# Order of the last group's down products, pinned operand splits and earlier loads in an encoder layer's MLP

## The chip, the cores and the metric

The kernel runs on one core of a Trainium2 chip. The metric is the device time of one execution in microseconds. TensorE (PE in the profile) multiplies matrices, VectorE (DVE), ScalarE (ACT) and GpSimd (POOL) work on elements, and SyncE (SP) issues most transfers (DMAs); GpSimd issues those transfers that add into their destination.

## The reference

One layer of an encoder on 1024 tokens of 1024 channels, in fp32, and what matters here is its gated MLP (D_FF = 2816):

```python
hn = rmsnorm(h, norm_ffn_g[i])
up = hn @ w_up[i]
gt, val = up[..., :D_FF], up[..., D_FF:]
gt = causal_dwconv(gt, conv_w[i], conv_b[i])
h = h + (jax.nn.gelu(gt, approximate=False) * val) @ w_down[i]
...
gate = jax.nn.sigmoid(hn @ w_ple_gate[i] + b_ple_gate[i])
h = h + gate * (p[i] @ w_ple[i])
```

Before it stand a pooling mixer, a chunked attention and the output projection.

## The kernel before, in words

Every fp32 product is made of three matmuls of fp32r halves (`mm3`, L128 to L130: high by high, high by low, low by high). An operand is first *split*: ScalarE copies it to its high half (L133), VectorE subtracts that for the low half (L134). The order of TensorE's instructions is the program's; on the other engines a scheduler orders them, by the data they wait for and by a priority (`tc.high_priority` puts an instruction ahead). SP and GpSimd work their queues of transfers strictly in the resulting order.

The MLP works in 22 tiles `fi` of 128 of D_FF's channels. Both of its products are made by a seven-product scheme for two by two blocks (Strassen's, in a form that needs few sums), so that seven block products stand for eight; they are numbered 1 to 7.

*Up products.* For a tile, step `n` is product `n` of the block scheme, 12 matmuls of 128x512. `order` lists all steps: four are done ahead, those of tile 0 follow in the order 6 3 7 4, of tile 1 in 5 6 2 7 3 4, of the others in 1 5 6 2 7 3 4. `prepare` makes the operand of a step up to four steps ahead: `fetch` loads the blocks of w_up into six buffers `rawu` (L695), as many steps ahead as its argument says and as far as buffers are free; `summed` adds blocks on VectorE (L699), then the operand is split. `step` runs the twelve matmuls into a bank of PSUM and then what follows: `keep` (L784) copies a bank to SBUF, `seed` (L788) copies a bank to another as the start of its sum, `gate` makes the convolution on ScalarE and VectorE (L833 to L835) and the Gelu (L836), `values_in` multiplies gate and value (L841, L843). Tiles in `halved` do the gate in two halves of 512 tokens, the others in one of 1024. The first Gelu needs another table of ScalarE's functions, loaded just before it.

*Down products.* The finished rows of tiles 0 to 19 are stored in DRAM (`Yd`), and w_down's product over them is made in five groups `g` of four tiles. Product `(g, n)` has 24 matmuls. Its operands are sums of quarters of w_down and `Yd`, made by the transfers: `ask` loads the first part plainly from SP and adds the others by accumulating DMAs of GpSimd (both recorded at L942 or L940), into the buffers RW. Products 5, 6 and 3 have buffers of their own in which the sum *grows*: product 6 adds to what product 5 had, and product 3 to that of 6 on the side of w_down. The others share one set. A buffer is asked anew when its last product has been split, and a row of `Yd` only when its tile is stored (`stored`). `split_next` splits the operands of the next product (L133 and L134, and L972 and L973 where the sign is turned), into the tiles BQ and four pieces of R; `down_next` runs the product, adds the four results to the residual (L990), and calls `split_next` for the one after. The hooks of `up` place one or more down products between the steps of a tile (`downs`). Products of a group go in the order 1 2 5 4 6 7 3.

*The end of the MLP.* Tiles 20 and 21 need no DRAM; their w_down rows, and the operands of the product of p and w_ple, are late pieces, loaded and split through the `rawu` buffers by `late_pair` (L1041), in hooks of tile 21 and after it. The last group's seven products lie in tiles 19 (three of them), 20 and 21.

Of the kernel before, what the change touches and what calls it, by code (L numbers as in the profile page):

```python
# [59 lines left out]
DOWN_ORDER = (1, 2, 5, 4, 6, 7, 3)  # L60
# [33 lines left out]
def trunk(tc, xT, pT, vecs, w_qk0, w_in, w_v, bias, counts, pool_w, w_out, w_up, w_down,  # L94
# [4 lines left out]
    with tc.tile_pool(name="sb", bufs=1) as sb, \  # L99
# [32 lines left out]
        def split(src, hi, lo):  # L132
            act.activation(hi, src, AF.Copy)  # L133
            dve.tensor_tensor(lo, src, rv(hi), ALU.subtract)  # L134
# [506 lines left out]
        out_weights(0, pooled)  # L641
        norm_a = Norm(HS[0], tmp[0], tmp[2:3], 6, 6)
# [28 lines left out]
        steps = {0: (6, 3, 7, 4), 1: (5, 6, 2, 7, 3, 4)}  # L671
# [29 lines left out]
        def prepare(upto):  # L701
            while prepared[0] < min(upto, len(order)):
                fi, n = order[prepared[0]]
                w_ = wu[prepared[0] % 3]
                prepared[0] += 1
                fetch(prepared[0] + 3)
                assert fetched[0] == len(loads) or loads[fetched[0]][0] >= prepared[0]
                if (fi, n) in alone:
                    t, = done_with = [held[(fi, n), q] for q in FORMS[n]]
                else:  # L710
                    a11, a12, a21, a22 = [held.get((fi, q)) for q in ((0, 0), (0, 1), (1, 0), (1, 1))]
                    if n == 5:
                        summed(a21, a21, a22)
                    elif n == 6:
                        summed(a21, a21, a11)
                    elif n == 3 and not fi:
                        summed(a11, a21, a12)
                    elif n == 7:
                        if fi:
# [3 lines left out]
                    done_with = {3: [a11, a12], 7: [a21], 4: [a22]}.get(n, []) if fi == 0 else {  # L723
                        3: [a11], 7: [a12, a21], 4: [a22]}.get(n, [])
# [55 lines left out]
        halved = (1, NF - 1)  # L780
# [9 lines left out]
        def step(fi, n):  # L790

            x, y, z, w = firsts.get(fi, (0, 1, 2, 3))
            product({1: x, 2: x, 5: z, 3: z, 6: y, 7: y, 4: w}[n], n in (1, 5) or (fi, n) == (0, 4))
# [16 lines left out]
            elif n == 7:  # L810
                if fi:
                    seed(w, y)
                else:
                    keep(V[:, HS[0]], y)
                dve.tensor_tensor(V[:, HS[1]], PS[:, y], p5, ALU.subtract)
            elif n == 4:
                if fi:
# [20 lines left out]
        def values_in(ts, negative=None):  # L838
# [6 lines left out]
            for h in range(2):  # L845
                y = Yb[:, HS[h]]
# [30 lines left out]
        def up(fi, dst, hooks=None):  # L877
# [30 lines left out]

        def sources(side, g, n):

            for j in range(2):
                if side == "w":
                    yield j, [w_down[group_of(g)[2 * k + j], :, i * 512:(i + 1) * 512] for i, k in DOWN_W[n]]
                else:
                    yield j, [Yd[group_of(g)[2 * k + j]][:, HS[t]] for k, t in DOWN_A[n]]
# [4 lines left out]
        def ask():  # L920
# [3 lines left out]
            for side in "wa":  # L924
                for kind in ("one", "grow"):
                    queue = todo_of[side, kind]
                    while queue:
# [3 lines left out]
                        if side == "a" and not all(group_of(g)[2 * k + j] in stored for k, _ in DOWN_A[n] for j in range(2)):  # L931
# [3 lines left out]
                        grown = n in (GROWING_W if side == "w" else GROWING_A)[1:]  # L935
# [9 lines left out]
        for side in "wa":  # L945
            for kind in ("one", "grow"):
                before, queue = None, []
                for g in range(5):
                    for n in DOWN_ORDER:
# [4 lines left out]
        sequence = [(g, n) for g in range(5) for n in DOWN_ORDER]  # L954
        nsplit, ndown = [0], [0]

        def split_next():
# [42 lines left out]
        for fi in range(4):  # L1000
# [15 lines left out]
            if fi == 2:  # L1016
# [5 lines left out]
                split_next()  # L1022
# [21 lines left out]
        def ple_weights():  # L1044
            for k in range(2):
                for z in HS:
                    late_pair(w_ple[k, :, z], wp[k][0][:, z], wp[k][1][:, z])

        def ple_rows(h):
            for k in range(2):  # L1050
                late_pair(pT[k, :, HS[h]], *pt[h][k])

        def down_weights(fi, dst):
            for z in HS:
                late_pair(w_down[fi, :, z], dst[0][:, z], dst[1][:, z])
# [52 lines left out]
        down_weights(last_f[0], wd2[0])  # L1108
        down_weights(last_f[1], wd2[1])
        ple_rows(1)  # L1110
# [167 lines left out]
```

## Time and profile before

| | us |
|---|---|
| median of 3 runs | 1145.96 |
| lowest and highest run | 1144.96 and 1147.01 |
| profiled execution | 1146.88 |
| its span | 1145.1 |
| TensorE busy | 1129.9 |
| VectorE busy | 888.2 |
| ScalarE busy | 604.7 |
| GpSimd busy | 146.8 |

The profile is of one execution; its times count from the start of its span, and the 1.8 us around the span are in the run's own time only. A row of the chain of waits gives start, duration and what ran; a row of the timeline gives start, duration, engine, line, operation and, in brackets, the idle time before it with what released it; a row of the windows gives a stretch, its length, the busy time of TensorE, of its weight loads, of VectorE, ScalarE and GpSimd (with counts), the granted clock of TensorE, the share of time that the 16 DMA engines are busy, and GB/s. Rows of transfers give their number, size and median time from issue to landing.

### The profile page before, as it was taken

The numbers are of one execution on the slowest core, as the hardware profiler recorded it, in microseconds if no ns is written. First come the engines' busy times: TensorE is split into PE (matmuls) and PEld (weight loads), VectorE is DVE, ScalarE is ACT, GpSimd is POOL, SyncE is SP. The second block draws the span as 40 slices with busy tenths as digits, with TensorE's granted clock in tenths as the row PEclk, the third lists the DMA queues.
The fourth block names the chain that finished last, engine by engine and source line by source line (L and its number), as shares of the span: only waits on it lengthen the run. The fifth ranks groups of instructions, "written<-read, shape, count | busy, mean of one in ns | idle before, by whom it ended". The sixth has DMA issues, their size and how long they took to land.

```text
span 1145.1 us, 15750 instructions
## 1 busy us (share of the span) xinstructions
PE 1129.9 (99%) x5675; PEld 958.2 (84%) x5675; DVE 888.2 (78%) x1541; ACT 604.7 (53%) x1068; POOL 146.8 (13%) x192
## 2 busy tenths in 40 slices
PE   9999999999999999999999999999999999999997
PEld 7988998888888778888888888888888887788897
DVE  7678878879658787888787878777887788986864
ACT  8568677765554554444444444443444344664644
POOL 0000000073002200120112011201120113000000
PEclk9999999999999999999999999999999999999999
DMA  7110101104500343575557655755575559320012
GB/s 265 37 49 31 50 12 68 40 28 151 172 19 10 97 128 117 140 172 140 144 144 162 158 148 146 173 141 145 152 172 138 145 148 183 114 92 19 1 74 74
DMA packets 65022, 125.89 MB, mean 110 GB/s; under 512 B 7344, under 2 KB 8624, under 8 KB 64944
## 3 DMA queue, kind: packets, MB, share of 16 engines
q1 hardware_dynamic: 50400, 98.60, 25.9%
q0 software_dynamic: 14400, 26.22, 14.1%
q8 instruction: 44, 0.72, 0.3%
q14 instruction: 34, 0.28, 0.1%
q10 hardware_dynamic: 144, 0.07, 0.0%
HBM read 110.18 MB, written 14.68 MB: 109 GB/s over the span
## 4 chain that ended last, share of the span: by engine, by line
PE 93%; issue 2%; ACT 2%; DMA 1%; DVE 1%; SPq 0%; POOL 0%; POOLq 0%; DVEq 0%; ACTq 0%
PE PS L128 28%; PE PS L129 28%; PE PS L130 28%; PE PS L367 2%; PE PS L385 1%; PE PS L384 1%; DMA F<-in_w_down 1%; PE PS L342 1%; PE PS L341 1%; DMA F<-in_w_qk 0%; PE PS L350 0%; PE PS L349 0%; PE PS L617 0%; DMA RW<-in_w_down 0%; ACT F L353 0%
## 5 line engine op out<-in xcount | busy, mean ns | idle before, releaser
L128 PE MATMUL PS<-R 128*128 128x512 f32 (+1 forms) x1176 | 443.2, 377 | 2.8 <-ACT F L784 2.1
L130 PE MATMUL PS<-R 128*128 128x512 f32 (+1 forms) x1176 | 438.4, 373 | 0.0
L129 PE MATMUL PS<-R 128*128 128x512 f32 (+1 forms) x1112 | 420.8, 378 | 0.3 <-DVE R L230 0.3
L128 PEld LDWEIGHTS PS<-R 128*128 128x128 f32 x1176 | 222.1, 189 | 40.7 <-ACT F L784 2.8
L130 PEld LDWEIGHTS PS<-R 128*128 128x128 f32 x1176 | 222.1, 189 | 39.1
L129 PEld LDWEIGHTS PS<-R 128*128 128x128 f32 x1112 | 210.0, 189 | 37.1 <-DVE R L230 0.9
L133 ACT ACTIVATE R<-F 128x512 fp32r<-128x512 f32 (+2 forms) x225 | 141.3, 637 | 186.1 <-PE PS L129 76.4
L134 DVE TENSOR_TENSOR R<-F,R 128x512 fp32r<-128x512 f32 (+2 forms) x221 | 152.8, 699 | 53.2 <-ACT R L133 52.3
L133 ACT ACTIVATE BQ<-RW 128x512 fp32r<-128x512 f32 x90 | 52.8, 623 | 85.5 <-PE PS L129 78.8
L990 DVE TENSOR_TENSOR F<-F,PS 128x512 f32<-128x512 f32 x140 | 92.3, 680 | 4.4 <-PE PS L130 4.3
L699 DVE TENSOR_TENSOR F<-F 128x512 f32<-128x512 f32 x88 | 60.5, 687 | 44.1 <-DMA F<-in_w_up 41.0
L940 POOL DMA_DIRECT2D RW<-Yd x60 | 52.4, 873 | 267.2 <-DMA RW<-Yd 215.2
L940 POOL DMA_DIRECT2D RW<-in_w_down x40 | 36.1, 951 | 227.1 <-DMA RW<-in_w_down 190.1
L134 DVE TENSOR_TENSOR BQ<-RW,BQ 128x512 fp32r<-128x512 f32 x90 | 59.1, 684 | 5.6 <-ACT BQ L133 4.3
L129 PE MATMUL PS<-BQ 128*128 128x512 f32 x140 | 54.9, 392 | 2.7 <-DVE BQ L973 2.7
L353 ACT ACTIVATE F<-F,small 128x640 f32<-128x640 f32 (+2 forms) x64 | 44.4, 693 | 21.1 <-DVE small L351 13.1
L128 PE MATMUL PS<-BQ 128*128 128x512 f32 x140 | 54.8, 392 | 0.3 <-ACT BQ L972 0.3
L128 PE MATMUL PS<-R,BQ 128*128 128x512 f32 x140 | 55.0, 393 | 0.0
L129 PE MATMUL PS<-R,BQ 128*128 128x512 f32 x140 | 54.9, 392 | 0.0
L130 PE MATMUL PS<-BQ 128*128 128x512 f32 x140 | 54.8, 391 | 0.0
L130 PE MATMUL PS<-R,BQ 128*128 128x512 f32 x140 | 54.7, 391 | 0.0
L609 ACT ACTIVATE F<-F 128x512 f32<-128x512 f32 (+1 forms) x49 | 27.9, 569 | 44.6 <-DVE F L1145 16.7
(186 smaller groups left out, 1803.0 us busy)
## 6 DMA issues: line engine op xcount, KB each, us to landing
F<-in_w_up SPq DMA_DIRECT2D x91, 256.0 KB, 4.2
RW<-Yd SPq DMA_DIRECT2D x60, 256.0 KB, 3.7
RW<-Yd POOLq DMA_DIRECT2D x60, 256.0 KB, 5.1
RW<-in_w_down SPq DMA_DIRECT2D x50, 256.0 KB, 2.8
RW<-in_w_down POOLq DMA_DIRECT2D x40, 256.0 KB, 6.2
Yd<-F SPq DMA_DIRECT2D x40, 256.0 KB, 2.4
F<-in_w_in SPq DMA_DIRECT2D x10, 512.0 KB, 3.5
F<-in_xT SPq DMA_DIRECT2D x16, 256.0 KB, 5.8
```

What stands on the lines that cost most here:

```text
L128: pe.matmul(ps, ahi, bhi, start=first, stop=False, skip_group_check=more)
L129: pe.matmul(ps, ahi, blo, start=False, stop=False, skip_group_check=more)
L130: pe.matmul(ps, alo, bhi, start=False, stop=last, skip_group_check=more)
L133: act.activation(hi, src, AF.Copy)
L134: dve.tensor_tensor(lo, src, rv(hi), ALU.subtract)
L341: pe.matmul(PS[:, 4 + z, 0:320], q, K2[:, ks], start=True, stop=False)
L353: act.activation(S[:, 0:n], S[:, 0:n], AF.Exp, bias=s_[:, 0:1], scale=-1.0, accum_out=s_[:, 1:2])
L367: pe.transpose(pst[:, j * P:(j + 1) * P], S[:, j * P:(j + 1) * P], ident)
L609: act.activation(self.q, src, AF.Square)
L699: dve.tensor_tensor(rawu[to], rawu[a], rawu[b], op)
L940: pool.dma_start(t, src, accum_op=ALU.add)
L990: dve.tensor_tensor(t, t, PS[:, 4 + d], ALU.subtract if n in (1, 5) else ALU.add)
```

## The change

Six things change.

1. The last group's order is 1 2 6 5 4 7 3. What grows is worked out from the order by a new function `parts`: product 6, which no longer follows product 5, is loaded as a whole sum (three parts on either side), product 5 from its own parts, and product 3's side of w_down from all four parts anew. That is 14 transfers of 256 KB more, 8 of them accumulating.
2. `split` can be pinned: its two instructions keep their place in the program's order. Pinned are the splits of product 1 of the first group, which the program calls behind tile 2, and those of the late pieces.
3. Tile 19 is halved, and its first half of tokens is stored before the second is made; `stored` knows halves.
4. Tile 1 runs its steps as 5 2 6 3 7 4, and takes its sums and its step 7 as tile 0 does.
5. `fetch` reaches six steps ahead for the first seven operands, where it reached three.
6. A Gelu of one column in the attention part (near 300 us) takes the table load ahead. The late pieces are asked and split in other hooks: two at step 5 of tile 21, four at step 6, four at step 7 and two at step 4, each with its own buffer in a list of twelve.

```diff
-DOWN_ORDER = (1, 2, 5, 4, 6, 7, 3)
+DOWN_ORDER = ((1, 2, 5, 4, 6, 7, 3),) * 4 + ((1, 2, 6, 5, 4, 7, 3),)
...
-        def split(src, hi, lo):
-            act.activation(hi, src, AF.Copy)
-            dve.tensor_tensor(lo, src, rv(hi), ALU.subtract)
+        def split(src, hi, lo, pinned=False):
+            both = (act.activation(hi, src, AF.Copy),
+                    dve.tensor_tensor(lo, src, rv(hi), ALU.subtract))
+            if pinned:
+                for i in both:
+                    tc.keep_in_program_order(i)
...
+        tc.keep_in_program_order(act.activation(small[:, 2:3], mhalf, AF.Gelu))
...
-        steps = {0: (6, 3, 7, 4), 1: (5, 6, 2, 7, 3, 4)}
+        steps = {0: (6, 3, 7, 4), 1: (5, 2, 6, 3, 7, 4)}
...
-                fetch(prepared[0] + 3)
+                fetch(prepared[0] + (3 if prepared[0] > 7 else 6))
...
-        halved = (1, NF - 1)
+        halved = (1, NF - 3, NF - 1)
...
-                values_in(slice(0, SEQ), dst)
-                for ts in HS:
-                    sp.dma_start(Yd[fi][:, ts], Yb[:, ts])
-                stored.add(fi)
-                ask()
+                for part in [HS[0:1], HS[1:2]] if fi == NF - 3 else [HS]:
+                    values_in(slice(part[0].start, part[-1].stop), dst)
+                    for ts in part:
+                        sp.dma_start(Yd[fi][:, ts], Yb[:, ts])
+                        stored.add((fi, HS.index(ts)))
+                    ask()
...
+        def parts(side, g, n):
+
+            own, growing = (DOWN_W, GROWING_W) if side == "w" else (DOWN_A, GROWING_A)
+            if n not in growing:
+                return own[n], False
+            at = growing.index(n)
+            if at and DOWN_ORDER[g].index(growing[at - 1]) < DOWN_ORDER[g].index(n) and (
+                    at < 2 or parts(side, g, growing[at - 1])[1]):
+                return own[n], True
+            return sum((own[m] for m in growing[:at + 1]), ()), False
...
-        def split_next():
+        def split_next(pinned=False):
...
-                        split(t, hi, lo)
+                        split(t, hi, lo, pinned)
...
-                split_next()
+                split_next(True)
...
-        late = [rawu[(nl + z) % 6] for z in (0, 1)]
-        nlate = [0]
-
-        def late_pair(src, hi, lo):
-            t = late[nlate[0] % len(late)]
-            nlate[0] += 1
-            sp.dma_start(t, src)
-            split(t, hi, lo)
+        late = [rawu[(nl + z) % 6] for z in (0, 1, 5, 3, 2, 0, 1, 5, 3, 4, 2, 0)]
...
+        def late_pairs(n):
+            for _ in range(n):
+                src, hi, lo = pieces[npiece[0]]
+                t = late[npiece[0]]
+                npiece[0] += 1
+                sp.dma_start(t, src)
+                split(t, hi, lo, True)
...
-        for n, fn in ((1, lambda: store(gv2[0])), (2, ple_weights), (3, lambda: ple_rows(0)),
-                      (4, lambda: late.extend(rawu[(nl + z) % 6] for z in (2, 3, 4, 5)))):
-            hooks.setdefault(n, []).insert(0, fn)
+        hooks.setdefault(1, []).insert(0, lambda: store(gv2[0]))
+        for n, many in ((5, 2), (6, 4), (7, 4), (4, 2)):
+            hooks.setdefault(n, []).insert(0, lambda many=many: late_pairs(many))
```

More of the change, by code (lines that the diff above doesn't have):

```diff
@@ L715, in prepare @@
                         summed(a21, a21, a11)
-                    elif n == 3 and not fi:
+                    elif n == 3 and fi < 2:
                         summed(a11, a21, a12)
                     elif n == 7:
-                        if fi:
+                        if fi > 1:
                             summed(a11, a21, a12)
@@ L792, in step @@
             x, y, z, w = firsts.get(fi, (0, 1, 2, 3))
-            product({1: x, 2: x, 5: z, 3: z, 6: y, 7: y, 4: w}[n], n in (1, 5) or (fi, n) == (0, 4))
+            product({1: x, 2: x, 5: z, 3: z, 6: y, 7: y, 4: w}[n], n in (1, 5) or n == 4 and fi < 2)
             if n == 1 and fi != 1:
@@ L845, in values_in @@
             for h in range(2):
+                if HS[h].stop <= ts.start or HS[h].start >= ts.stop:
+                    continue
                 y = Yb[:, HS[h]]
@@ L912, in sources @@
                 if side == "w":
-                    yield j, [w_down[group_of(g)[2 * k + j], :, i * 512:(i + 1) * 512] for i, k in DOWN_W[n]]
+                    yield j, [w_down[group_of(g)[2 * k + j], :, i * 512:(i + 1) * 512] for i, k in parts(side, g, n)[0]]
                 else:
-                    yield j, [Yd[group_of(g)[2 * k + j]][:, HS[t]] for k, t in DOWN_A[n]]
+                    yield j, [Yd[group_of(g)[2 * k + j]][:, HS[t]] for k, t in parts(side, g, n)[0]]
         def buffer(side, n):
@@ L930, in ask @@
                             break
-                        if side == "a" and not all(group_of(g)[2 * k + j] in stored for k, _ in DOWN_A[n] for j in range(2)):
+                        if side == "a" and not all((group_of(g)[2 * k + j], t) in stored for k, t in parts(side, g, n)[0] for j in range(2)):
                             break
```

33 lines of the change are left out of this document (14 added, 19 removed).

## The prediction

> **What bounds the kernel now.** I read the page's first parts, then what TensorE waits for, then the chain of waits in the two places where its waits are long, and last GpSimd's issues of DMAs there.
>
> ```profile
> PE 1129.9 (99%) x5675; PEld 958.2 (84%) x5675; DVE 888.2 (78%) x1541; ACT 604.7 (53%) x1068; POOL 146.8 (13%) x192
> ...
> PE 93%; issue 2%; ACT 2%; DMA 1%; DVE 1%; SPq 0%; POOL 0%; POOLq 0%; DVEq 0%; ACTq 0%
> ```
> ```profile
> PE PS L129 <- DVE BQ L973: 2.7, 2, 1.6
> PE PS L128 <- ACT F L784: 2.1, 1, 2.1
> ...
> PE PS L128 <- ACT PS L788: 0.7, 1, 0.7
> ```
> TensorE is the bound. The change leaves its 5675 matmuls as they are, so it can only take TensorE's waits away or add some. The three rows (total, times, longest) are its waits in the MLP. The chain shows the first place, around 394 and 406 us (start, duration, what):
>
> ```profile
> 390.89 3.75 DMA RW<-in_w_down
> ...
> 395.81 0.59 ACT F L784
> ...
> 397.07 0.43 PE PS L129
> ...
> 404.28 1.28 ACT L836
> 405.57 1.06 ACT F L836
> 406.63 0.49 ACT PS L788
> ```
> ```profile
> 393.76 0.60 PE L625 MATMUL PS<-ident,small 128*128 128x128 f32 x4
> 396.44 0.63 PE L128 MATMUL PS<-R 128*128 128x512 f32 x1 [2.08 <-ACT F L784]
> ```
> ```profile
> 406.10 0.39 PE L130 MATMUL PS<-R 128*128 128x512 f32 x1
> 407.17 0.50 PE L128 MATMUL PS<-R 128*128 128x512 f32 x1 [0.68 <-ACT PS L788]
> ```
> ```profile
> 397.00:400.00 3.00, 3.00 (x9) 2.32 (x8) 3.00 (x5) 1.45 (x3) 1.98 (x2) 0.50 0.86 276
> ```
> ScalarE was set to split a block of w_down that landed only at 394.64 (390.89 + 3.75), and the copy `keep` (L784) that frees the bank of tile 0's step 7 stood behind it: 2.1 us idle. Matmuls then run at 0.43 us instead of 0.23 for some 3.4 us (granted clock 0.50 in the window), which loses about 1.5. At 407.17 TensorE waited for a table load, a Gelu and a copy between banks. A warm matmul should follow after 0.23, so this loses 407.17 − 406.10 − 0.23 = 0.84. With some smaller lags I put the place at 5.0 us.
>
> The second place is the last group of down products:
>
> ```profile
> 954.04 0.39 PE L128 MATMUL PS<-BQ 128*128 128x512 f32 x1
> 955.55 0.50 PE L129 MATMUL PS<-BQ 128*128 128x512 f32 x1 [1.13 <-DVE BQ L973]
> ```
> ```profile
> 967.79 8.20 DMA F<-in_w_down
> 976.01 0.64 ACT R L133
> ...
> 980.65 0.43 PE PS L128
> ```
> ```profile
> 977.03 0.39 PE L130 MATMUL PS<-R 128*128 128x512 f32 x1
> 977.74 0.49 PE L128 MATMUL PS<-BQ 128*128 128x512 f32 x1 [0.33 <-ACT BQ L972]
> 979.83 0.50 PE L129 MATMUL PS<-BQ 128*128 128x512 f32 x1 [1.59 <-DVE BQ L973]
> ```
> Product 4 of the last group waits 955.55 − 954.04 − 0.23 = 1.3 us for VectorE's half of its late operand. Product 7 waits 0.48 + 1.86: ScalarE stood before a late piece of w_down, asked at 967.79 and landed at 975.99, though product 7's own operand was there. The clock then halves once more (0.43 at 980.65), about 1.5. With the lags this place is 5.4 us. So **the most that the change can bring is 5.0 + 5.4 = 10.4 us**, 0.9%.
>
> **The change part by part.** Region 1, tiles 0 to 2. The split of the first w_down block is pinned to its place in the program, behind tile 2, so `keep` no longer stands behind it and step 7 of tile 0 starts at about 394.2 instead of 396.44. With 12 matmuls at 0.227 a step (2.72 us), tile 0 step 4 starts at 396.9 and tile 1 step 5 at 399.6, ending at 402.4. The next step is tile 1's step 2 now; it may not overwrite its bank before the seed copy has read it, and that copy stands behind tile 0's Gelu.
>
> ```profile
> 396.73 0.33 SPq L695 DMA_DIRECT2D F<-in_w_up  x1
> ```
> ```profile
> 399.35 1.41 DVE L699 TENSOR_TENSOR F<-F 128x512 f32<-128x512 f32 x2
> ...
> 401.94 0.68 DVE L134 TENSOR_TENSOR R<-F,R 128x512 fp32r<-128x512 f32 x1
> 402.54 1.28 DVE L835 SCALAR_TENSOR_TENSOR F<-F,vec 128x1024 f32<-128x1024 f32 x1
> ```
> ```profile
> F<-in_w_up SPq DMA_DIRECT2D x91, 256.0 KB, 4.2
> ```
> These VectorE operations, the sums of w_up blocks first, end at 403.82 before. The earlier fetch asks the second block at about 393.4 instead of 396.73; by the median landing it is there at 397.6, and as other transfers share the engines I take 398.6. The same run of operations then starts some 0.7 earlier and ends at 403.1; the Gelu (1.06, its 1.28 table load taken ahead) ends at 404.2, and with 0.49 for the seed TensorE starts at 404.7 instead of 407.17: **2.4 us won**. The table load and a Gelu of one column now stand ahead of two bank copies near 300 us:
>
> ```profile
> 300.42 1.45 ACT L485 ACTIVATE F<-PS,small,vec 128x512 f32<-128x512 f32 x2
> ```
> ```profile
> 303.10 0.39 PE L128 MATMUL PS<-R 128*128 128x512 f32 x1
> ```
> The first copy is done at about 301.2, and TensorE takes its bank at 303.10; that 1.9 hides the some 1.4 us, so I cost it at nothing; without the cover it costs up to 1.4. But in region 1 there lies, between 402.4 and 404.7, an idle gap of 2.3 us, as long as the one that halved the clock at 396.44; where it does so again, 1.5 of the 2.4 goes. I put 0.6 on that: −1.5, between −0.9 and −2.4. The Trainium skill (page "TensorE: Matmul & The Clock Gate", section "Part 1: The HAM clock gate (the "warmup" mystery)") says that the clock drops after a whole idle window of about 3.4 us. By that the gap would be free and the sum would be 0.9 lower; the row above, half clock after 2.1 us of idleness, speaks against it, and I go by the row.
>
> Region 2. Tile 19 in halves puts two half operations (0.68 in the row at 401.94) more ahead of a split on VectorE near 916, which comes just in time there, and lets half 0 be stored earlier: nothing, up to 0.5 us. The hooks ask and split the late pieces one step ahead, with pinned splits, so product 7 should no longer stand behind them: of its 2.3 + 1.5 us I let 1 stay, **−2.8**. Against this stands GpSimd's queue. Group 4 runs 1 2 6 5 4 7 3. Product 6 is loaded as a sum of three parts, product 5 follows with its own sums, product 3 loads all four parts of w_down: 14 more DMAs of 256 KB, 8 of them accumulating on GpSimd.
>
> ```profile
> 933.42 0.86 POOL L940 DMA_DIRECT2D RW<-Yd  x1 [26.86 <-DMA RW<-Yd]
> 936.08 0.86 POOL L940 DMA_DIRECT2D RW<-Yd  x1 [1.80 <-issue]
> 939.90 0.89 POOL L940 DMA_DIRECT2D RW<-Yd  x1 [2.96 <-DMA RW<-Yd]
> 941.46 0.88 POOL L940 DMA_DIRECT2D RW<-Yd  x1 [0.67 <-DMA RW<-Yd]
> ...
> 946.55 0.88 POOL L940 DMA_DIRECT2D RW<-Yd  x1 [0.61 <-issue]
> ```
> ```profile
> RW<-Yd POOLq DMA_DIRECT2D x60, 256.0 KB, 5.1
> ```
> These are the two chains of sums for product 4's operands, one in RW at 8 (933.42, 939.90) and one in RW at 10 (936.08, 941.46, 946.55). Each link waits until the one before it has landed, 5.1 to 5.4 us on the second chain. In the changed kernel's order the second link of RW at 8 stands ahead of the first of RW at 10, so that chain starts 1.56 after 939.90, at 941.5, not at 936.08. **And the four accumulations of product 5, which TensorE now needs third from last but before product 4, stand behind the chain's last link.** By links of 5.1 the last is issued at 951.7; by 4 us (the transfers of product 6 are out of the way) at 949.5. I take 950. Four issues at 1.6 (from 939.90 to 941.46) put the fourth at 956.4, and with a landing of 4 to 5 it is there at about 960.5. Its split on ScalarE (0.6), then, next in its queue, a Gelu of 1.06 and an up split of 0.6, then two VectorE halves of 0.68, follow before the second matmul. Some of this overlaps: TensorE goes on at 962 to 963, where product 5's slot is 954.04. That is **8.5 us of stall, and 2.4 for one and a half windows of half clock, against the 1.4 of before: +9.5**. With links, issues and landings at their shortest (949.5, 1.4, 4) the stall is 6 and the part +6.5; with all at the longest it is 11 and the part +12.
>
> The rest of the added DMAs: 6 plain and 8 accumulating.
>
> ```profile
> q1 hardware_dynamic: 50400, 98.60, 25.9%
> q0 software_dynamic: 14400, 26.22, 14.1%
> ```
> ```profile
> 948.00:952.00 4.00, 4.00 (x20) 3.30 (x18) 4.00 (x6) 1.62 (x3) 1.74 (x2) 1.00 1.06 168
> ```
> Share times span by bytes gives 0.78 us of all 16 engines for a plain block and 1.6 for an accumulating one: 6 × 0.78 + 8 × 1.6 = 17 us, in a stretch where they are full in some slices already (1.06). Product 3 comes last, so its sums have the time of product 7 and the up steps behind it; I count nothing, with +5 as the bound (product 7 waiting behind the added sums on GpSimd). Everything between tile 2 and tile 18 keeps its order: nothing.
>
> **The sum**: −1.5 − 2.8 + 9.5 = +5.2 on the profiled execution's 1146.88, which is 1145.1 of span and 1.8 around it. A half microsecond I take off, since what the steps lose near 916 and 955 partly overlaps and late sums may land faster than the rows of a full stretch: +4.6. The median of the three runs is 1145.96, 0.9 below the profiled one, so I forecast **1150.5 us**.
>
> **Rivals.** (a) *The reordered group flows, faster* (0.25). If product 5's four sums have landed by about 952.5, the operand is split in time and no stall is left there. That takes the chain on RW at 10 some 8 us shorter than by my rows: for it speaks that product 6's transfers are gone from 944 to 953, against it that every link in the rows took over 5 us. The time is then 1145.96 − 1.5 − 2.8 − 1.3 = 1140.4; with no drop of the clock and nothing left at product 7, 1138.5, and 1135.6 is the bound. About 0.2% (2.3 us) is what a measurement of this kernel can tell from no change; the point from which this rival decides is a stall at product 5 below about 3.4 us without a drop of the clock (−1.5 − 2.8 + 3.4 − 1.4 = −2.3). (b) *It cancels* (0.13). A stall of 4 us with one halved window, +5.5 − 1.4 = +4, against −4: 1144 to 1148. (c) *The transfers become the bound* (0.12). The added 17 us push the sums of products 7 and 3 back, and product 7 waits 5 us more, again with a drop: 1145.96 + 4.6 + 6 = 1156.5. For it speaks the 8.20 us of the late piece at 967.79, against it that these pieces are asked a step ahead now. (d) *The change doesn't do what it says in region 1*: the pins leave the copy late, 5 us stay, and the time is 1152; within the forecast's case.
>
> **How the numbers follow.** The forecast 0.50, (a) 0.25, (b) 0.13, (c) 0.12. So faster by over 0.2% 0.25, within 0.2% 0.13, slower 0.62. The forecast's own range is 1148.3 to 1154, from the shortest and longest chain. For 8 in 10 the range reaches into (a) and up to (c): 1139 to 1156.
>
> **What would show it.** Right: TensorE's longest wait lies at product 5 of the last group, 6 us or more near 954, released by an ACT or DVE operation behind a DMA into RW, with the clock at 0.5 after it; GpSimd's accumulations for it issued after 949; the wait for L784 at 394 gone; TensorE's wait near 403 about 2 us; none of the late pieces ahead of product 7. Wrong: those four sums landing before 953; or a first wait near 394 still there; or product 7 as the longest wait.

## The result and the profile after

| | before | after |
|---|---|---|
| median, us (5 runs each) | 1145.96 | 1166.19 |
| lowest and highest | 1144.96 and 1147.01 | 1164.96 and 1166.97 |
| span of the profiled execution | 1145.1 | 1164.4 |

The changed kernel takes 1.0175 of the time before (95% interval 1.016 to 1.0189): slower, as forecast, but by 20 us instead of 4.6, and outside the range of 1139 to 1156. The page of the changed kernel, its engines and the chain that ended last by engine:

```profile
PE 1133.6 (97%) x5675; PEld 959.7 (82%) x5675; DVE 889.7 (76%) x1544; ACT 604.9 (52%) x1071; POOL 154.1 (13%) x200
...
PE 83%; DVE 5%; issue 4%; DMA 4%; ACT 2%; POOL 1%; SPq 0%; POOLq 0%; DVEq 0%; ACTq 0%
```

The matmuls are the same, but TensorE's share falls from 99% to 97% of a longer span. What it waits for (total, times, longest, in us):

```profile
PE PS L128 <- ACT BQ L133: 7.1, 1, 7.1
PE PS L129 <- DVE BQ L134: 5.9, 2, 5.4
PE PS L128 <- ACT BQ L990: 2.5, 1, 2.5
PE PS L128 <- ACT PS L792: 1.9, 1, 1.9
...
PE PS L128 <- ACT R L990: 1.3, 1, 1.3
PE PS L129 <- DVE R L991: 1.1, 1, 1.1
```

TensorE's timeline, at tile 1, at the last group's product 5 and at its product 7, says where these lie:

```profile
405.46 0.50 PE L128 MATMUL PS<-R 128*128 128x512 f32 x1 [1.86 <-ACT PS L792]
```
```profile
962.36 0.80 PE L128 MATMUL PS<-BQ 128*128 128x512 f32 x1 [7.10 <-ACT BQ L133]
968.56 0.80 PE L129 MATMUL PS<-BQ 128*128 128x512 f32 x1 [5.40 <-DVE BQ L134]
```
```profile
994.78 0.50 PE L128 MATMUL PS<-BQ 128*128 128x512 f32 x1 [2.48 <-ACT BQ L990]
...
997.55 0.79 PE L128 MATMUL PS<-R,BQ 128*128 128x512 f32 x1 [1.32 <-ACT R L990]
999.40 0.79 PE L129 MATMUL PS<-R,BQ 128*128 128x512 f32 x1 [1.06 <-DVE R L991]
```

Each of the three is followed by half clock (the column before the last two of the windows: 0.51, 0.50, 0.50):

```profile
406.00:409.00 3.00, 3.00 (x9) 2.30 (x8) 3.00 (x6) 0.44 (x1) 0.00 (x0) 0.51 0.16 45
...
969.00:972.00 3.00, 3.00 (x8) 2.32 (x8) 3.00 (x6) 0.00 (x0) 0.87 (x1) 0.50 0.96 227
1000.00:1003.00 3.00, 3.00 (x9) 2.32 (x8) 2.18 (x4) 3.00 (x6) 0.00 (x0) 0.50 0.19 68
```

TensorE runs the same 5675 matmuls in the same places, so the start of the n-th in one trace less its start in the other shows where the time went. This *lag* of the changed kernel behind the kernel before is 1.0 at 380 us, −0.1 at 900, 0.9 when the third product of the last group starts (943.4 before), 14.9 within the fourth (960), 19.15 at the seventh (992) and 19.15 at the end: 1.0 at the start of the kernel, −1.1 in tiles 0 to 2, 1.0 at product 6, 14.0 at product 5 with its half clock, 4.3 at product 7 with its own.

What made product 5 late is seen in GpSimd's queue of accumulating transfers (start, duration, operation, idle time before):

```profile
933.54 0.86 POOL L958 DMA_DIRECT2D RW<-Yd  x1 [3.28 <-DMA RW<-Yd]
939.93 1.78 POOL L958 DMA_DIRECT2D RW<-Yd  x2 [5.53 <-DMA F<-in_w_down]
...
947.12 0.86 POOL L958 DMA_DIRECT2D RW<-Yd  x1 [2.19 <-DMA RW<-Yd]
952.53 0.86 POOL L958 DMA_DIRECT2D RW<-Yd  x1 [4.55 <-DMA RW<-Yd]
953.14 2.07 POOL L958 DMA_DIRECT2D RW<-in_w_down  x2
956.91 0.86 POOL L958 DMA_DIRECT2D RW<-Yd  x1 [1.70 <-issue]
958.94 0.89 POOL L958 DMA_DIRECT2D RW<-Yd  x1 [1.17 <-issue]
965.56 0.88 POOL L958 DMA_DIRECT2D RW<-in_w_down  x1 [5.73 <-DMA RW<-in_w_down]
...
983.28 0.86 POOL L958 DMA_DIRECT2D RW<-in_w_down  x1 [4.49 <-DMA RW<-in_w_down]
...
990.75 0.86 POOL L958 DMA_DIRECT2D RW<-Yd  x1 [3.78 <-issue]
```

Against the rows of before: product 4's second link for RW at 8 and first for RW at 10 go together at 939.93 (the latter was at 936.08), the chain's last link at 952.53 (946.55), and behind it product 5's four sums from 953.14 to 958.94. Product 3's six follow from 965.56, and product 7's four, from 983.28 to 990.75, come last of all. The chain of waits from the fourth sum of product 5 on:

```profile
958.94 6.04 DMA RW<-Yd
...
965.62 1.04 ACT F L840
966.66 0.53 ACT R L133
...
967.82 0.70 DVE BQ L134
...
968.56 0.80 PE PS L129
```

Landed at 964.98, its split, then a Gelu, an up split and VectorE's half of another operand stand between it and TensorE: the path that the prediction named, 5.6 to 6.6 us later than it put it.

The chain of waits into product 7 starts with the last split of product 4's operand on the side of w_down:

```profile
977.23 0.70 DVE BQ L134
...
977.94 6.60 DMA RW<-in_w_down
...
985.18 1.79 POOL RW L958 x2
986.97 3.78 issue
990.75 6.01 DMA RW<-Yd
...
996.87 0.63 ACT R L990
```

Product 7 uses the buffers of product 4, its neighbour now, so its plain loads can be asked only when product 4 has been split. They land from 982.64 to 986.00, and its sums follow them; product 3's sums are not on this chain. The fourth sum is held back for another 3.78 us, which the profile calls "issue" (theory D below says what they are). TensorE comes to product 7 at 992.30; it waits for the third sum, landed at 994.07, and then for the fourth, landed at 996.76.

### The profile page after: what moved, and what is told of

It reads as the page before. It is cut to its first block, busy times and chain, and to the rows that moved or that the text cites. A ratio compares the mean times of both kernels' runs of the same rounds, so it can differ in the third digit from the quotient of the medians.

```text
span 1164.4 us, 15779 instructions
## 1 busy us (share of the span) xinstructions
PE 1133.6 (97%) x5675; PEld 959.7 (82%) x5675; DVE 889.7 (76%) x1544; ACT 604.9 (52%) x1071; POOL 154.1 (13%) x200
## 4 chain that ended last, share of the span: by engine, by line
PE 83%; DVE 5%; issue 4%; DMA 4%; ACT 2%; POOL 1%; SPq 0%; POOLq 0%; DVEq 0%; ACTq 0%
PE PS L129 25%; PE PS L128 25%; PE PS L130 25%; PE PS L370 2%; DVE R L134 2%; DMA RW<-Yd 2%; PE PS L388 1%; PE PS L387 1%; DMA F<-in_w_up 1%; POOL RW L958 1%; PE PS L345 1%; PE PS L344 1%; ACT R L133 1%; DMA RW<-in_w_down 1%; DMA F<-in_w_qk 1%
## 5 line engine op out<-in xcount | busy, mean ns | idle before, releaser
L958 POOL DMA_DIRECT2D RW<-in_w_down x46 | 41.2, 963 | 238.9 <-DMA RW<-in_w_down 203.3
L837 ACT ACTIVATE F<-F,vec 128x1024 f32<-128x1024 f32 (+1 forms) x25 | 28.6, 1143 | 47.4 <-DVE F L812 44.6
```

Source lines behind the costliest of these rows:

```text
L837: act.activation(y, Gb[:, 2 + a:2 + b], AF.Identity, bias=vec[:, C_CB + fi:C_CB + fi + 1], scale=cw(2))
L958: pool.dma_start(t, src, accum_op=ALU.add)
```

## The experiments

Each lag below is that of the n-th matmul behind the kernel before, in the profiled execution, as the difference over a piece: the start of the kernel, tiles 0 to 18, and, in the last group, the third, the fourth, and the fifth to seventh product. The start differs from execution to execution by up to 2.5 us in kernels that are the same there, and says nothing about an edit. The lags are those of one execution, which lies up to 3.3 us from its kernel's median (e10_5_first_pinned: 1164.38).

The expectations weigh theories, by letters. A: products that are neighbours in the order share a set of buffers, so that their loads have less time. B: the pinned splits and the late pieces' new places cost the time. C: the 14 added transfers fill the DMA engines. D: a sum is late by its place in GpSimd's queue, which has few transfers in flight. E: the place in that queue alone counts. F (in e11_later_w_down only): one late block of w_up sets the gap in tile 1.

| kernel | median, us | of before (95%) | start | tiles 0-18 | third | fourth | fifth to seventh |
|---|---|---|---|---|---|---|---|
| after | 1166.19 | 1.0175 (1.016-1.0189) | 1.0 | −1.1 | 1.0 | 14.0 | 4.3 |
| e1_old_order | 1152.14 | 1.006 (1.0039-1.0081) | −0.1 | −1.0 | 0.1 | 7.6 | −2.6 |
| e2_alternate | 1153.67 | 1.0062 (1.0039-1.0086) | 0.9 | −0.8 | 2.1 | 0.0 | 6.7 |
| e3_order_only | 1157.85 | 1.0102 (1.0066-1.0138) | 1.1 | −0.8 | 0.0 | 11.0 | −2.2 |
| e4_no_sums_5 | 1156.83 | 1.0086 (1.0055-1.0117) | 0.7 | −2.1 | 0.0 | −0.1 | 8.3 |
| e5_turns_old_order | 1145.15 | 1.0001 (0.9989-1.0013) | 0.3 | −1.0 | 0.0 | −1.5 | −1.0 |
| e6_turns | 1161.6 | 1.0133 (1.0109-1.0156) | 0.6 | −2.5 | 0.2 | 11.9 | 4.0 |
| e7_5_first | 1166.17 | 1.0185 (1.0163-1.0207) | 0.5 | −0.3 | 0.5 | 14.4 | 3.8 |
| e8_no_sums_4 | 1154.27 | 1.008 (1.0057-1.0103) | 0.4 | −3.0 | 0.1 | 1.2 | 7.1 |
| e9_half_sums | 1144.14 | one run | 0.3 | 0.4 | 0.0 | 0.7 | −4.1 |
| e10_5_first_pinned | 1167.71 | 1.018 (1.0159-1.02) | 0.3 | −1.9 | 0.0 | 1.4 | 17.3 |
| e11_later_w_down | 1144.28 | 0.9977 (0.9966-0.9988) | 0.0 | −4.9 | 0.4 | −0.1 | 2.1 |
| e12_whole_19_old_order | 1147.81 | 1.0012 (1.0-1.0025) | 2.3 | −0.3 | 0.0 | −0.2 | −0.5 |
| e13_best | 1143.78 | 0.9978 (0.9966-0.9989) | 0.6 | −4.7 | 0.6 | 0.2 | 1.9 |
| e14_7_before_3 | 1157.78 | 1.0099 (1.0083-1.0116) | 0.8 | −2.4 | 0.0 | 1.9 | 10.2 |

**e1_old_order.** Is it the order alone?

```diff
-DOWN_ORDER = ((1, 2, 5, 4, 6, 7, 3),) * 4 + ((1, 2, 6, 5, 4, 7, 3),)
+DOWN_ORDER = ((1, 2, 5, 4, 6, 7, 3),) * 5
```

> The changed kernel with the last group back in the order 1 2 5 4 6 7 3, all else as changed. Theory A (the new order puts products that share a set of operand buffers side by side: 6 and 5, then 4 and 7, so their loads, a plain one and accumulating ones in series, have one slot of about 12 us instead of two): the 14.9 us at product 5 and the added 4.3 us at product 7 go, and what is left against before is region 1 (-1.1) and the late pieces off product 7 (-3 to -4): 1141 to 1143 us. Theory B (the pinned splits and the late pieces' new places cost product 7 its time): product 7 still waits 5 us or more, 1148 us or more.

Measured 1152.14: neither. Product 7 is freed as theory A says (−2.6), so theory B falls in the old order; e6_turns comes back to it in the new one. But the fourth product, here product 4, loses 7.6. GpSimd's queue holds its chains in the changed kernel's order also here, the first for RW at 10 not until the second for RW at 8 (939.27, two issues in one row):

```profile
932.74 0.86 POOL L958 DMA_DIRECT2D RW<-Yd  x1 [27.59 <-DMA RW<-Yd]
939.27 1.78 POOL L958 DMA_DIRECT2D RW<-Yd  x2 [5.67 <-DMA F<-in_w_down]
...
950.32 0.86 POOL L958 DMA_DIRECT2D RW<-Yd  x1 [3.73 <-DMA RW<-Yd]
```

**e3_order_only.** The other way round: the kernel before with the new order, `parts` and nothing else.

```diff
-DOWN_ORDER = (1, 2, 5, 4, 6, 7, 3)
+DOWN_ORDER = ((1, 2, 5, 4, 6, 7, 3),) * 4 + ((1, 2, 6, 5, 4, 7, 3),)
...
```

> The kernel before with the last group's new order and its sums loaded anew, and nothing else of the change. Theory A: 15 us at product 5 and some 4 at product 7 come in by the order alone: 1163 to 1167 us, TensorE waiting 12 us or more at product 5. Theory B: the order alone costs less than 8 us, below 1154.

1157.85, between the two. The order costs 11 at product 5, less than in the changed kernel since GpSimd's turns are those of before here (936.26 for RW at 10). Product 7 loses nothing, although it shares its buffers with product 4 and has its sums behind product 3's six here too.

**e2_alternate.** The new order, but neighbours never share buffers.

```diff
-        def buffer(side, n):
-            return "grow" if n in (5, 6, 3) else "one"
+        def buffer(side, n, g):
+            return "grow" if n in ((5, 6, 3) if g < 4 else (6, 4, 3)) else "one"
...
```

> The changed kernel with its new order and all its transfers, but in the last group product 5 takes the buffers of the set that 1, 2, 4 and 7 use, and product 4 those of 6 and 3, so that neighbours in the order never share a set. Theory A: the loads have two slots again, the waits at products 5 and 7 go to under 2 us each, 1142 to 1147 us. Theory C (the 14 added transfers fill the DMA engines, whichever buffer they go to): 1158 us or more.

1153.67, between. Product 5 loses nothing, so the added bytes alone (C) don't hold it up. The edit does two things at once, though: product 5 no longer shares buffers with product 6, and its four sums now go ahead of product 4's six on GpSimd (930.30 to 940.01). It can't tell theory A from the place in the queue; e8_no_sums_4 and e10_5_first_pinned can. And 6.7 us come in at products 4 and 7: the wait has moved.

**e4_no_sums_5** leaves out product 5's four accumulations.

```diff
                             for z, src in enumerate(srcs):
+                                if (g, n) == (4, 5) and z:
+                                    continue
```

> The changed kernel, but the last group's product 5 gets only the first part of each of its four operands (its four accumulating transfers are left out, so part of the sum is missing). Theory A: the plain loads land around 951 us, so the wait at product 5 goes from 14 us to under 2, that at product 7 stays (4 to 8 us): 1149 to 1154 us. Theory C: four transfers less give back some 6 us of the engines' time, 1159 to 1161 us.

1156.83, above A's 1149 to 1154 and below C's 1159. Product 5 waits for nothing, so its plain loads were in time and the sums were late; product 7 still loses 8.3.

So a theory D, on GpSimd's queue: a sum stands behind another chain's waiting link, and few transfers are in flight. In all sixteen traces (before, after and fourteen experiments) an accumulating transfer is never issued before the one three places ahead has landed: of the 97 such pairs in the kernel before the closest is 0.31 us after the landing, and 25 lie 0.25 to 0.45 us after it. In the changed kernel (issue and landing from the trace's own events):

```
sum            issued   landed   waits in its own program for
product 4, 6th 952.53   956.60   the link before, landed 952.14
product 5, 1st 953.14   958.63   a load landed 947.20
product 5, 2nd 953.75   959.93   a load landed 948.05
product 5, 3rd 956.91   961.57   a load landed 950.06    (956.60 + 0.31)
product 5, 4th 958.94   964.98   a load landed 950.87    (958.63 + 0.31)
```

With three in flight and a median of 5.6 us from issue to landing in the changed kernel, GpSimd brings in one sum in some 1.9 us (an estimate, 5.6 / 3). The profile names this wait "issue", or an unrelated VectorE operation.

**e9_half_sums** asks what is counted: the kernel before with every accumulating transfer in two halves.

```diff
-                                    pool.dma_start(t, src, accum_op=ALU.add)
+                                    for c in (slice(0, 256), slice(256, 512)):
+                                        pool.dma_start(t[:, c], src[:, c], accum_op=ALU.add)
```

> The kernel before with each of its 100 accumulating transfers of 256 KB issued as two of 128 KB. If the three in flight are three transfers, an issue still never starts before the one three places earlier has landed, the pairs of halves take longer than one whole, and sums come late at many products: 1155 us or more. If the limit counts bytes or packets, six are in flight and the time is 1145 to 1150 us.

Transfers are counted: of 197 issues none goes before the landing three places ahead, and 142 go 0.25 to 0.45 us after it. But the expected price was wrong: a half lands in a median of 3.7 us against 5.4 for a whole one over all 100, and with chains that move on sooner the one run took 1144.14, no slower.

**e5_turns_old_order** is e1 with product 4's six sums issued in turns.

```diff
+                        both = [(z, j, src) for j, srcs in sources(side, g, n) for z, src in enumerate(srcs)]
+                        if (g, n) == (4, 4):
+                            both.sort(key=lambda b: b[:2])
...
+                                i = pool.dma_start(t, src, accum_op=ALU.add)
+                                if (g, n) == (4, 4):
+                                    tc.keep_in_program_order(i)
```

> The kernel of e1_old_order (all of the change but the new order), with GpSimd's six accumulations for product 4 of the last group issued in turns, one for RW at 8, one for RW at 10, and so on, as the kernel before had them; in e1 the first for RW at 10 stood behind the second for RW at 8, was issued at 939.88 and the chain landed at 955.78. Theory D (GpSimd's queue: a sum behind another chain's waiting link, and no more than three accumulating transfers in flight, as every trace so far shows): the first for RW at 10 goes at about 936, the chain lands at about 952, product 4's wait falls from 7.0 us to 1.5 to 2.5 and its half clock goes, and the late pieces' gain at product 7 is seen: 1141 to 1144 us where before gives 1145.5. Theory B (late pieces and halves of tile 19 delay the operand themselves): product 4 still waits 5 us or more, 1149 us or more.

```profile
933.65 0.86 POOL L960 DMA_DIRECT2D RW<-Yd  x1 [1.90 <-issue]
936.11 0.89 POOL L960 DMA_DIRECT2D RW<-Yd  x1 [1.60 <-DMA RW<-Yd]
938.76 0.88 POOL L960 DMA_DIRECT2D RW<-Yd  x1 [1.76 <-DMA RW<-Yd]
941.33 0.86 POOL L960 DMA_DIRECT2D RW<-Yd  x1 [1.70 <-DMA RW<-Yd]
944.02 0.86 POOL L960 DMA_DIRECT2D RW<-Yd  x1 [1.83 <-issue]
```

The first for RW at 10 goes at 933.65, the last at 944.02 instead of 950.32, and the 7.6 us at the fourth product turn into −1.5: e1's 7 us were the order of six issues, as theory D says. The median, 1145.15, is above D's 1141 to 1144 and does not differ from before. The trace ends 3.1 us ahead of that of before, with 1.0 of it where the late pieces' gain was expected, in the fifth to seventh product; single runs of both kernels spread over 5 us here.

**e12_whole_19_old_order** is e1 with tile 19 whole, nothing pinned on GpSimd.

```diff
-        halved = (1, NF - 3, NF - 1)
+        halved = (1, NF - 1)
...
-                for part in [HS[0:1], HS[1:2]] if fi == NF - 3 else [HS]:
+                for part in [HS]:
```

> The kernel of e1_old_order with tile 19 made whole again, nothing pinned on GpSimd. With tile 19 whole the scheduler gives GpSimd's queue the turns that the kernel before had; in e1 it does not. Theory D: the 7 us of e1 over e5 go without any pin, 1143 to 1146 us, product 4 waits under 2.5 us. Theory B (the late pieces' new places): product 4 still waits 5 us or more, 1149 us or more.

1147.81, 1.8 above D's range, with a start 2.3 later than before's in the profiled execution. The fourth product loses nothing (−0.2), and GpSimd has the turns of before. So it was the halving of tile 19 that made the scheduler swap them.

**e6_turns** is the changed kernel with e5's edit (the same diff, in the new order).

> The changed kernel in its new order, with the same six accumulations for product 4 in turns. Theory D: the chain ends 4 us sooner and so product 5's four sums behind it, the wait at product 5 falls from 14 us to about 10 and that at product 7 stays: about 1162 us. Theory A alone (neighbours that share buffers): product 4's chain has no part in it, 1165 to 1167 us.

1161.6, the time that D gave. The fourth sum for product 5 lands at 960.49 instead of 964.98; as this execution comes to product 5 some 2.6 us sooner, product 5 still loses 11.9 instead of 14.0, where D had about 10.

Set beside e3, this run also bears on theory B. GpSimd's queue has the same order in both, but product 7 loses 4.0 here and nothing in e3. What differs is the rest of the change: eight late pieces are asked from 976.95 to 985.78 here, beside product 7's loads and sums, and two in e3. The four sums take 5.9 to 8.1 us to land here and 4.2 to 6.5 in e3. No run moves the late pieces alone in the new order, so that they are the cause is likely and not shown.

**e7_5_first** meant to put product 5's sums ahead of product 4's, by asking product 4's operands later.

```diff
-                for kind in ("one", "grow"):
+                for kind in ("grow", "one") if (side, 4, 6) in split_done else ("one", "grow"):
...
+                        if (g, n) == (4, 4) and (side, 4, 6) not in split_done:
+                            break
```

> The changed kernel, but product 4's operands of the last group are asked only when product 6's have been split, behind those of product 5, so that product 5's four sums stand first in GpSimd's queue. Theories A and D together: product 5's plain loads still start only after product 6's split and land at 947 to 951, its sums go at 947.5 to 953.5 and land by about 959.5, so that a wait of 6 to 9 us stays at product 5; product 4's sums follow with three in flight and land at 971 to 974, product 4 waits up to 4 us, product 7 as before: 1157 to 1164 us. Theory E (only the place in GpSimd's queue counts): product 5 waits less than 3 us, 1155 us or less.

1166.17, as after; GpSimd's queue came out as before the edit, product 4's sums first, so this run tells nothing of its question. **e10_5_first_pinned** keeps e7's edit, issues product 4's six in turns as e5 does, and holds the order by pins.

```diff
...
+                                    i = pool.dma_start(t, src, accum_op=ALU.add)
+                                    if g == 4 and n in (4, 5):
+                                        tc.keep_in_program_order(i)
```

> The changed kernel with its new order, GpSimd's queue held to this order by pins: product 5's four sums, then product 4's six in turns (in e7_5_first the scheduler had put product 4's ahead all the same). Theories A and D together: product 5's plain loads still start when product 6 has been split and land at 947 to 951, its sums go at 947.5 to 953 and land by about 958.5, the wait at product 5 is 6.5 to 8.5 us instead of 12.5 in the profile's waits; product 4's sums land by 971 and hold it up little; product 7 waits as before: 1157 to 1161 us. Theory E (only the place in GpSimd's queue counts): product 5 waits less than 3 us, 1154 us or less. If the wait stays over 11 us, the queue's order is not what made product 5 late.

Product 5 loses 1.4 and waits 2.5 us, less than A and D together gave (6.5 to 8.5), and as theory E had it (under 3), though its buffers are shared as before. So at product 5 the place in GpSimd's queue was the cause. E's time, 1154 or less, fails: at 1167.71 the kernel is no faster than the changed one. Of the 17.3 us in the fifth to seventh product 5.1 stand at product 4, whose six sums follow product 5's now, and 12.2 at product 7. The waits of products 5 and 7, and GpSimd's first issue for product 5 and its last one:

```profile
PE PS L128 <- ACT BQ L997: 10.6, 1, 10.6
PE PS L129 <- DVE BQ L134: 2.5, 1, 2.5
```
```profile
941.73 0.86 POOL L963 DMA_DIRECT2D RW<-in_w_down  x1 [12.48 <-DMA RW<-in_w_down]
...
989.80 0.86 POOL L963 DMA_DIRECT2D RW<-Yd  x1 [1.36 <-DMA F<-in_pT]
```

Product 7's last sum goes at 989.80 (990.75 after). Twenty sums, for products 4, 5, 3 and 7, stand in this queue in either order, where the kernel before has fourteen up to product 7's last; product 7 gets its own at the end of all twenty.

**e14_7_before_3** is e10 with product 7's four sums ahead of product 3's six, in the order of use, and product 3's in turns; the sums of both are pinned too.

```diff
+            turns = [("w", "one"), ("a", "one"), ("w", "grow"), ("a", "grow")]
...
+                        if (g, n) == (4, 3) and ("a", 4, 4) not in split_done:
+                            break
...
```

> The kernel of e10_5_first_pinned, with product 7's four sums ahead of product 3's six in GpSimd's queue and product 3's in turns: the order of use, 5, 4, 7, 3. In e10 product 7's last sum was issued at 989.80 behind product 3's and landed at 994.41. Theory D with the order: product 7's sums go at 966 to 976 and land by 981, its wait falls from 14 us with its half clock to 4 to 6, product 3's sums land by about 996, just in time: 1152 to 1157 us. Theory of supply alone (20 sums take the same time in any order, the wait moves on to product 3): 1162 us or more. Theory A (product 7's plain loads, late because it shares buffers with product 4, set its time): 1158 to 1163 us.

1157.78, 10 us below e10, between D's range and theory A's (0.8 above the one, 0.2 below the other). The order among the sums is thus about half of e10's loss. In the trace product 7's 12.2 us fall to 2.0; 5.2 stay at product 4 and 3.0 come in at product 3. The chain of waits into product 3 runs through the split of product 4's operand and product 7's loads:

```profile
967.23 0.70 DVE BQ L134
...
967.95 5.64 DMA RW<-in_w_down
...
974.24 2.67 POOL RW L969 x3
976.91 4.93 issue
981.85 6.28 DMA RW<-in_w_down
```

Product 7's second load is asked at 967.95, right behind the split of product 4's operand, and each of product 7's sums of w_down goes 0.6 us after its load has landed: here the shared buffers (A) count. The 4.93 us behind them are D's again, since product 3's first sum goes 0.31 us after the landing three places ahead (981.54).

**e8_no_sums_4** leaves out product 4's six accumulations in the changed kernel.

```diff
                             for z, src in enumerate(srcs):
+                                if (g, n) == (4, 4) and z:
+                                    continue
```

> The changed kernel without the six accumulations for product 4 of the last group (five sixths of its operand's sums are missing, so part of the result is left out); everything else in the changed kernel's order. By supply at 1.9 us a sum, six sums less give 11 us: product 5's sums start when its loads land, at 947.5, and land at 957 to 959, it waits 5 to 7 us, and product 7's sums come 8 to 11 us sooner: 1152 to 1156 us. By shared buffers alone the waits at 5 and 7 stay near 6 and 5 us with their half clock: 1157 to 1160 us.

1154.27, in the range that supply gave: six sums less bring 12 us. They don't come where supply had them. Product 5 waits 2.4 us and not 5 to 7, because its sums go from 940.73 on and not from 947.5; its buffers are shared as before, so they were not what held it. Product 7 still loses 7.1, with its loads landed by 969.82 and its first sum at 970.81, right behind product 3's sixth (970.21).

**e11_later_w_down** is e5 with four loads of w_down for the first group behind the w_up blocks that tile 1 waits for.

```diff
-                sp.dma_start(rawu[i], w_up[fi, v, :, z * 512:(z + 1) * 512])
+                fetches.append(sp.dma_start(rawu[i], w_up[fi, v, :, z * 512:(z + 1) * 512]))
...
+                            elif side == "w" and (g, n) in ((0, 1), (0, 5)):
+                                with tc.issue_after(fetches[-1].ins):
+                                    sp.dma_start(t, src)
```

> The kernel of e5_turns_old_order with the four plain loads of w_down for the first group issued behind the loads of w_up for tiles 1 and 2; in e5 they stand before the block of w_up that landed at 398.77, and VectorE, and through it the Gelu, the seed and TensorE at 402.67, waited for that block. Theory F (that block alone sets the gap in tile 1): it lands near 396.3, the chain of the gate runs 2 us or more sooner, TensorE's gap there goes from 2.0 us to under 0.7 and the half clock behind it goes: 2 to 3.5 us below e5. Rival: the chain of the gate waits for something else there (the bank copy or the convolution), and the gap stays over 1.5 us, same time as e5.

VectorE's sum of the two w_up blocks and the gate behind it, in e5 and then in e11:

```profile
398.87 1.42 DVE L703 TENSOR_TENSOR F<-F 128x512 f32<-128x512 f32 x2 [2.61 <-DMA F<-in_w_up]
400.20 1.28 DVE L838 SCALAR_TENSOR_TENSOR F<-F,vec 128x1024 f32<-128x1024 f32 x1
```
```profile
395.83 1.41 DVE L704 TENSOR_TENSOR F<-F 128x512 f32<-128x512 f32 x2
397.23 1.28 DVE L839 SCALAR_TENSOR_TENSOR F<-F,vec 128x1024 f32<-128x1024 f32 x1
```

The 2.61 us of waiting are gone, TensorE's gap at 402.5 and its half clock with it, and tiles 0 to 18 give back 4.9 of the 5.0 us that the prediction had put there. Theory F holds in its place; in time e11 is 0.9 below e5 in the medians and 2.8 in the ratios to before, where F gave 2 to 3.5. At 0.9977 this is faster than before, but in the last group 2.4 us come in, since the products are due 4 us sooner and their sums are not.

**e13_best** is e11 with e12's edit (tile 19 whole):

> All of the change but the new order and the halves of tile 19, with GpSimd's six sums in turns and the first group's w_down loads behind w_up of tiles 1 and 2 (e11 with tile 19 whole). If the halves of tile 19 bring nothing of their own, the time is that of e11 within 1 us; if they make product 2 or 4 of the last group early, e11 is 1 us or more faster.

1143.78 against 1144.28, the same; the halves of tile 19 bring nothing. Both are below the kernel before by 0.2%, with intervals that leave 1 out.

## Why the prediction was wrong

- *The direction, and the mechanism at product 5*: right. Product 5's four sums stood behind product 4's chain, and TensorE's longest waits were there, released by ACT and DVE behind a DMA into RW.
- *Product 5, +9.5*: 14.0. The chain on RW at 10 began 1.0 earlier than put (940.51), but its links took 6.6 and 5.4 us from issue to issue, more than the 5.1 of the longer bound, and the last went at 952.53, not 950. "Four issues at 1.6" took the 6.4 us that they were put at (952.53 to 958.94), for another reason: the third and fourth waited for landings, and the spacing of 1.56 that the prediction took was a wait for a landing as well. The landing took 6.0 instead of 4 to 5. Together 4.5 us late at the landing, 964.98 against 960.5, which is the 4.5 us of the error.
- *Product 7, −2.8*: **the step that failed**. Product 7 was to be free once the late pieces went ahead of it, and for its own operand the prediction counted nothing, with +5 as the bound. It lost 4.3: of the 15.7 us between 1150.5 and 1166.19, 7.1 lie here and 4.5 at product 5. In the changed kernel its buffers came free at 977.93, with product 4's split; the loads, the sums and the wait for a place in flight took until 996.76, where TensorE came to the product at 992.30. Where product 5 is made early (e8, e10) product 3's six, ahead of product 7's on GpSimd, hold it up instead: with the sums in the order of use its loss falls from 12.2 (e10) to 2.0 (e14). "Product 3 comes last, so its sums have the time" took the order of use for the order of the queue. The late pieces themselves, asked earlier, likely add to it: with the new order and the old places (e3) product 7 loses nothing. Rival (c) had the place and, by its 1156.5, half of the size; its reason, the bytes, is at most a part: e14 moves the bytes of e10 in 10 us less.
- *Product 6*, for which the prediction has no term: 1.0 in this execution, 0.0 to 0.5 in e7, e10 and e14, which have the same order.
- *Region 1, −1.5*: −1.1. The copy L784 no longer waits; the gap was forecast at 2.3 us (402.4 to 404.7) and is 2.0 (405.46 − 403.21 − 0.23; the profile has 1.86), at a start 1.0 us later. The clock halved behind it, to which the prediction gave a chance of 0.6. Of eleven kernels with this gap, six show it and five don't. The Trainium skill (page "TensorE: Matmul & The Clock Gate", section "Part 1: The HAM clock gate (the "warmup" mystery)") speaks of a free-running window, which fits that the same gap halves the clock in one execution and not in another. That a whole window of about 3.4 us must be idle does not agree with the 0.51 granted after an idle time of 1.86.
- *The Gelu of one column near 300 us*, put at nothing: nothing; the changed kernel's lag is 0.99 at 300 and at 310 us.
- *Tile 19 in halves, nothing up to 0.5*: right in TensorE's own terms, but in the old order it cost 4.3 us in the medians (e1 against e12), and 7.8 at the fourth product in the traces, by what the scheduler made of GpSimd's queue.
- *Start*: +1.0, by chance. The half microsecond taken off the sum (which gives +4.7, not +4.6) stands on nothing that the runs show.

What is not settled: in the order of use (e14) 10 us remain, 5.2 of them at product 4, and how much of them is shared buffers, supply by GpSimd or full DMA engines was not separated; whether the late pieces' new places cause product 7's loss in the new order; and why product 7 gains 2.6 in e1 and 1.0 or less in e5 and e12, with the same instructions for it.

## What to carry to other kernels

A queue that works strictly in order, with few transfers in flight, is an engine with a rate of its own: count what stands in it up to each due time, for every product behind the edit and not only for the first, and take freeing one wait as moving it until the last due time holds. When an order of use is changed, look at which neighbours share buffers and how long after the release an operand can be there, and put the transfers into the order of use as well. Where a scheduler decides, a small edit in one engine's work (tile 19's halves) can swap another engine's queue, and the queue's new order, not the edit, sets the price.

## What the runs showed of the hardware

GpSimd had at most three accumulating transfers in flight, counted in transfers and not in bytes: in sixteen traces no issue goes less than 0.25 us after the landing of the one three places ahead, with wholes of 256 KB (some 1.9 us a sum, an estimate from 5.6 us to landing) as with halves of 128 KB. TensorE's clock fell to half (0.51 granted) after 1.9 us of idleness in one execution (after) and stayed at 1.00 after 2.4 in another (e10_5_first_pinned).
